# Sums of squares of k and q by products with a block of ones in place of squares with running sums, with a new order of both mixing stages

## The chip, the cores and the metric

One core of a Trainium2 chip. The metric is the device time of one execution in microseconds (us), the median of several runs. The engines are TensorE (PE, products; its loads of weights are PEld), VectorE (DVE), ScalarE (ACT), GpSimd (POOL) and SyncE (SP), which issues the transfers.

## What is computed

Two layers of a decoder trunk over 512 positions of width 1024, in fp32. Each layer first mixes positions by three groups of heads that share one projection in and one out, then runs a gated feed-forward part:

```python
for i in range(DEPTH):
    h = rms_norm(x, attn_pre_norm[i])
    z = h @ w_in[i]
    aq, ak, av, conv_u, gdn_qkv, gdn_gate, gdn_a, gdn_b = jnp.split(z, offsets, axis=-1)
    y_attn = dilated_attention_mixer(aq, ak, av, positions)
    y_conv = conformer_conv_mixer(conv_u, ...)
    y_gdn = gated_deltanet_mixer(gdn_qkv, gdn_gate, gdn_a, gdn_b, ...)
    mix = jnp.concatenate([y_attn, y_conv, y_gdn], axis=-1)
    x = x + rms_norm(mix @ w_out[i], attn_post_norm[i])
    h = rms_norm(x, ffn_pre_norm[i])
    f = (jax.nn.silu(h @ w_gate[i]) * (h @ w_up[i])) @ w_down[i]
    x = x + rms_norm(f, ffn_post_norm[i])
```

The change is in the gated delta rule (4 heads of 128 channels). There k and q pass a short convolution over positions, and each position's vector is scaled to length one:

```python
def l2_normalize(t):
    return t * lax.rsqrt(jnp.sum(t * t, axis=-1, keepdims=True) + L2_EPS)
```

The sums of squares that this needs, one for each position and head, are what the change computes in another way.

## The kernel before, in words

**Layout.** Activations lie channel by channel: a tile has 128 channels as partitions and 512 positions. Dense products take a block of weights of 128x128 against 128x512 of activations; each is done as three products of rounded and remaining parts (h0h with wh, h0h with wl, h0l with wh, for instance). Weights come in units of four blocks, in one fixed order: SP issues the transfer (wr, 256 KB), ACT casts the rounded part (wh), DVE, for some units POOL, subtracts the rest (wl). A unit is twelve products of 128x512.

**The order.** The code does not run as it is written. Every operation is recorded in a plan (`add`, L310) with a cost (`cost`, L267); `forward` (L420) then simulates the engines and writes out one static order for each, always taking the ready operation of highest rank. A rank is the longest path to the end, in which each engine's durations are stretched by the table STRETCH (one for each layer, L143), plus a bonus of the segment (tables BONUS and DENSE, L140 and L141). `issue` (L607) issues that order, so nearly every instruction has line 625. Queues of SP run in the order written. Two things are added by the plan itself: loads of ACT's function tables (L622) where the next function needs another table, and dummies, products `fill` of 128x256 (L1472), where PE has nothing ready and had little work in the time just before.

**A layer's mixing stage.** Its segments are K, Q, V (the delta rule's three inputs), S (its chain over chunks), O (its output), A and B (attention), C (convolution), G (gates) and W (a part of the out-projection, run early). For each head K takes a projection z, `short_conv` (tile kT), four transposes of kT into PSUM (pkt), the sums of squares (`sum_squares`, L1027), and a copy of pkt to SBUF (ktok). From all heads' sums ssk come rk and lrk, from these the rows of decay (prw, pbc, em) and the gram products pkk. The sums acm of their blocks are negated on ACT (acn), go out by two transfers (rows) and come back by 16 transfers as aext, 16 partitions each. DVE then solves a triangular system in 16 steps (sbt, pext), which ends with the last pext. K4 and K5 (tm, pc, c, pd, inner) and the chain S (pvn, pks, pso) follow. In segment Q each head's qT was transposed only for its squares (pqt), then ssq, rq and the rows of q follow. The attention turns its inputs by 4 times 4 transfers between tiles in SBUF (azs) with tables (tab) for the rotation; its last products pao go through DVE (ao) and transposes (paT) into the out-projection.

**The sums before.** For a head, `sum_squares` takes the four 128x128 blocks of the transposes in PSUM, positions as partitions, and ACT squares each and sums it along the row into one column of ssk or ssq (`accum_out`). Each such activation is followed in the records by a read of the accumulator.

Of the kernel before, what the change touches and what calls it, by code (L numbers as in the profile page):

```python
# [11 lines left out]
AF = mybir.ActivationFunctionType  # L12
# [4 lines left out]
S = 512  # L17
# [5 lines left out]
NC = S // 128  # L23
# [3 lines left out]
Q0, K0, V0, U0, G0, GG0, AB0 = 0, 256, 512, 768, 1280, 2816, 3328  # L27
# [109 lines left out]

BONUS = [{'K': 8577.3, 'K1': 1744957.2, 'K2': 999490.1, 'K7': 1081252.3, 'K3': 487102.8, 'K4': -30177.1, 'K5': 114036.9, 'C1': -967277.0, 'Q': 241547.0, 'Q1': 493634.3, 'V': 1059007.4, 'A': 180739.3, 'A1': 662680.2, 'A2': 504358.5, 'S0': 448057.0, 'S1': 509056.5, 'S2': 672779.4, 'S3': 1764589.9, 'O0': 452154.1, 'O1': 482497.0, 'O2': -115387.4, 'O3': 645125.1, 'B3': -55969.7, 'G3': 362503.2, 'C0': -73387.1, 'CN': 684240.7, 'G1': -1321750.9, 'B1': -352050.7, 'B2': -146055.8, 'G2': -444738.8, 'G0': -655720.9, 'B0': -644551.8, 'W': 1406690.3}, {'K': 437659.4, 'K1': 8288.2, 'K2': -21573.9, 'K7': -232713.7, 'K3': 265981.0, 'K4': 64171.9, 'K5': -138460.3, 'Q': -61445.2, 'Q1': -134753.1, 'C1': -196798.2, 'V': 282017.6, 'S0': 956554.0, 'S1': 1194914.1, 'S2': 160050.7, 'S3': 572915.2, 'O0': 624293.1, 'O1': 698094.8, 'O2': -189061.5, 'O3': 501707.8, 'C0': -124334.4, 'CN': 708987.6, 'A': -1560620.8, 'A1': -523695.9, 'A2': -871924.7, 'G0': 1312117.5, 'G3': 241949.4, 'G1': -1313223.2, 'B1': -215325.5, 'G2': -29759.2, 'B2': 632260.6, 'B0': -902903.6, 'B3': -419790.2, 'W': 853551.8}]  # L140
DENSE = [{'K': 1838801.0, 'K1': 1570972.6, 'K2': 1585654.0, 'K7': 1708264.2, 'K3': 1596435.1, 'K4': 2065165.3, 'K5': 1653043.4, 'C1': 2619907.9, 'Q': 639660.4, 'Q1': 623713.0, 'V': -184996.8, 'A': -509056.1, 'A1': -146920.5, 'A2': -488748.4, 'S0': 1317670.9, 'S1': 14477.9, 'S2': 1190644.3, 'S3': 869876.2, 'O0': 602389.2, 'O1': 1207172.3, 'O2': 939331.5, 'O3': 1308009.2, 'B3': -401133.5, 'G3': -21773.3, 'C0': 227567.6, 'CN': -61979.2, 'G1': -372988.3, 'B1': -346176.6, 'B2': -521887.3, 'G2': -365397.0, 'G0': 146413.7, 'B0': 870828.5, 'W': 1037753.1}, {'K': -301790.3, 'K1': -182758.9, 'K2': 1541.0, 'K7': -116696.3, 'K3': 157311.4, 'K4': -227839.6, 'K5': -215982.6, 'Q': -387096.1, 'Q1': 580637.9, 'C1': 26292.9, 'V': 63698.0, 'S0': 100432.3, 'S1': 142318.5, 'S2': 9579.0, 'S3': 420199.1, 'O0': -549345.1, 'O1': -33017.9, 'O2': -638243.5, 'O3': -260264.6, 'C0': 708601.5, 'CN': 579740.9, 'A': -274083.2, 'A1': 249147.9, 'A2': -28643.0, 'G0': -192252.3, 'G3': 500853.9, 'G1': -6303.9, 'B1': 496445.6, 'G2': 490543.7, 'B2': 208435.8, 'B0': -219860.5, 'B3': 165475.0, 'W': 294526.2}]  # L141

STRETCH = [{'PE': 0.1589, 'ACT': 1.5061, 'DVE': 0.9834, 'POOL': 0.0}, {'PE': 0.7128, 'ACT': 2.5956, 'DVE': 2.4432, 'POOL': 0.1292}]  # L143
QUOTA = {'z': 8, 'cm': 2, 'as': 6, 'scm': 2}
TUNE = {'wtop': 1, 'wbonus': 0.0, 'stick': 4000, 'force': 0, 'spread': 2.8, 'low': 2900, 'fill': 5000, 'warm': 12, 'early': 0, 'hib': 2000.0, 'raw': 4, 'half': 12000.0, 'taps': 14, 'plo': 4, 'hold': 1000, 'passes': 0, 'S': 78, 'P': 7, 'Q': 5, 'ahead': 5, 'more': 6, 'n_out': 4, 'n_ffn': 6, 'n_down': 2, 'n_in': 8}

# [111 lines left out]
class Plan:  # L258
# [8 lines left out]
    def cost(self, op, eng, name, outs, ins, kw):  # L267
        if eng == "SP":
            v = (outs + ins)[0]
            op.data = (v.p1 - v.p0) * v.size * 4 / 360  # L270
            if ins and ins[0].tail:
                op.data *= TUNE["spread"]
            return 475
        o = outs[0]
        if eng == "PE":
            if name == "transpose":
                return 62 if ins[0].p1 - ins[0].p0 <= 64 else 112
            w, m = ins[0], ins[1]
            if w.buf.dt == F32R:
                return max(112, 13 + m.size * 0.4167)  # L280
            k, c = w.p1 - w.p0, w.size
            if k == 64 and c == 128:
                return 110 + 0.84 * m.size
            if max(k, c, m.size) <= 64:
                return 62 if max(k, c, m.size) <= 32 else 114
            return max(224, m.size * 1.676)
        n = max([v.size for v in ins] + [o.size])
        psum = any(v.buf.pool.kind == "PSUM" for v in outs + ins)
        if eng == "ACT":
            d = FIXED[eng] + 0.832 * n - 42 * psum  # L290
            d += 93 * sum(isinstance(kw.get(x), View) for x in ("scale", "bias"))
            d += 93 * ("accum_out" in kw)
            return d
        if eng == "DVE":
            per = 1.042
            scalars = op.args[2:4] if name in ("tensor_scalar", "scalar_tensor_tensor") else ()
            if name == "scalar_tensor_tensor":
                scalars = scalars[:1]
            if name in ("tensor_scalar", "tensor_copy", "memset") and not psum:
                per = 0.521  # L300
            if name == "reciprocal":
                per = 8.3
            if name == "tensor_reduce":
                per = 1.8
            ptr = any(isinstance(v, View) for v in scalars)
            return FIXED[eng] + per * n + 9 * ("accum_out" in kw) + 61 * ptr
        per = 3.28 if name == "tensor_copy" else 1.0 if name == "memset" else 4.19 if name == "tensor_scalar" else 2.1
        return FIXED[eng] + per * n
# [319 lines left out]
def trunk(nc, tc, xT, wst, wab, par, con, big, out, depth=DEPTH, dbg=None):  # L628
# [3 lines left out]
    V, A, G, T, SP = (plan.engine(e) for e in ("DVE", "ACT", "POOL", "PE", "SP"))  # L632
    with ExitStack() as ctx:
# [12 lines left out]
        def slot(shape, dt=F32, name="s"):  # L646
            t = slots.tile(shape, dt, name)
            if name in QUOTA:
                t.buf.quota = (name, QUOTA[name])
            return t  # L650
# [4 lines left out]
        def bank(shape=(128, S), name="pb"):  # L655
            t = banks.tile(shape, F32, name)
            if name in QUOTA:
                t.buf.quota = (name, QUOTA[name])
            return t
# [33 lines left out]
        ones = cn[:, C_ONE:C_ONE + 128]  # L693
# [211 lines left out]
        for layer in range(depth):  # L905
# [42 lines left out]
            for seg in SEGMENTS[layer]:  # L948
# [5 lines left out]
                if seg == "K":  # L954
# [66 lines left out]
                    def token_major(src, name):  # L1021
                        ps = bank((128, NC, 128), name=name)
                        for n in range(NC):
                            T.transpose(ps[:, n], src[:, 128 * n:128 * (n + 1)], ident)
                        return ps

                    def sum_squares(ps, dst):  # L1027
                        junk = slot([128, NC, 128], name="junk")
                        for n in range(NC):
                            A.activation(junk[:, n], ps[:, n], AF.Square, accum_out=dst[:, n, :])  # L1030

                    s8r = table(B_S8, "s8", True)

# [2 lines left out]
                    kT, ktok, kkp = [], [], []  # L1036
                    ssk = small([128, NC, 4], "ssk")
                    for hd in range(NH):
                        kT.append(short_conv(project(), 1, hd))
                        ps = token_major(kT[hd], "pkt")  # L1040
                        sum_squares(ps, ssk[:, :, hd:hd + 1])
                        t = slot([128, NC, 128], name="ktok")
                        A.copy(t, ps)
                        ktok.append(t)
# [163 lines left out]
                if seg == "Q":  # L1208

                    qT = []  # L1210
                    ssq = small([128, NC, 4], "ssq")
                    for hd in range(NH):
                        qT.append(short_conv(project(), 0, hd))
                        sum_squares(token_major(qT[hd], "pqt"), ssq[:, :, hd:hd + 1])
                    stage("Q1")
                    rq = small([128, NC, 4], "rq")
                    colq = small([128, NC, 4], "colq")
                    small_rstd(rq, ssq, 1.0, [128, NC, 4], colq)
                    V.scalar_tensor_tensor(colq, colq, -0.5 * math.log(128.0), gcen, op0=OP.add, op1=OP.add)
                    rqe = small([128, NC, 4], "rqe")  # L1220
                    V.scalar_tensor_tensor(rqe, rq, 128.0 ** -0.5, eg, op0=OP.mult, op1=OP.mult)
                    rowq = rows_of(colq, "q")
                    iT = []
                    for hd in range(NH):
                        eq, last = decay(rowq, hd, 1, "eq", inner[:, 1, hd])
                        V.tensor_tensor(eq, gram(kT[hd], qT[hd], "pkq", last), eq, op=OP.mult)
                        iT.append(eq)
                    show("iT0", iT[0])
# [320 lines left out]
```

## Time and profile before

| | |
|---|---|
| median of 3 runs | 1343.43 us (1342.97 to 1344.2) |
| the profiled execution's own time | 1345.2 us |
| its span | 1343.4 us |
| granted clock of TensorE, mean | 0.987 |
| moved by the transfers | 118.50 MB, mean 88 GB/s |
| dense products pmm, share of the chain that ended last | 79% |
| splits wl on DVE | 378, 261.1 us busy |
| casts wh on ACT | 400, 227.6 us busy |

The chain that ended last is followed back from the last instruction, at each step to what released it. In groups of instructions, a row names line, engine, operation, output and inputs, shape and count; then the busy time, the mean of one in ns, and the idle time of the engine just before them with what ended it. In pieces of the timeline, a row holds the start in us from the span's start, the length, the engine and what ran; a bracket holds the idle time before it and what ended that.

Layer 0 runs its mixing stage from some 20 to 255 us and layer 1 from some 690 to 925; between and behind them stand the out-projections and the feed-forward parts.

### The profile page before, as it was taken

What the parts mean: (1) busy time and instruction counts of PE and PEld (TensorE: products, weight loads), DVE (VectorE), ACT (ScalarE), POOL (GpSimd) and SP (SyncE); (2) the same over time, 40 slices, a digit from 0 to 9 for tenths busy, and PEclk for the clock granted to TensorE, in tenths of its full rate; (3) what the DMA queues carried; (4) which work ended last, traced back from release to release, by engine and by line L of the source; (5) the groups of instructions that cost most, each with busy time, mean ns of one, the idle gap of its engine ahead of it and who ended that gap; (6) DMA issues with size and microseconds to landing.
All of it is one profiled execution on the core that took longest, in us unless ns stands there. A gap on an engine that the chain in (4) does not pass through costs nothing.

```text
span 1343.4 us, 20505 instructions
## 1 busy us (share of the span) xinstructions
PE 1314.9 (98%) x7501; PEld 1130.4 (84%) x7501; DVE 824.4 (61%) x1731; ACT 641.5 (48%) x1515; POOL 169.6 (13%) x134
## 2 busy tenths in 40 slices
PE   9999999999999999999999999999999999999996
PEld 8988779789888888878999888878898888888886
DVE  7686989669433444724497999774874334455324
ACT  5785368756222222524358777656642222253321
POOL 1086131100000000000001476310000000000000
PEclk9999989999999999999999979999999999999998
DMA  6064200423323231332301510405133222213311
GB/s 250 9 158 124 89 2 25 141 64 103 94 87 102 89 92 55 109 112 93 116 28 43 155 33 25 141 24 163 43 118 94 98 91 87 88 46 125 108 42 63
DMA packets 64437, 118.50 MB, mean 88 GB/s; under 512 B 8016, under 2 KB 8784, under 8 KB 64336
## 3 DMA queue, kind: packets, MB, share of 16 engines
q1 hardware_dynamic: 64336, 117.19, 28.1%
q8 instruction: 59, 0.97, 0.3%
q14 instruction: 42, 0.34, 0.1%
HBM read 112.70 MB, written 2.36 MB: 86 GB/s over the span
## 4 chain that ended last, share of the span: by engine, by line
PE 89%; DVE 6%; ACT 3%; DMA 1%; issue 1%; POOL 0%; SPq 0%; DVEq 0%; ACTq 0%; POOLq 0%
PE pmm L625 79%; PE pao L625 1%; DVE ca L625 1%; PE pas L625 1%; PE pss L625 1%; PE pso L625 1%; PE pap L625 1%; PE pc L625 1%; PE pkq L625 1%; PE pab L625 1%; PE pd L625 1%; PE pbc L625 1%; DMA x<-in_xT_dram 0%; ACT junk L625 0%; DVE sct L625 0%
## 5 line engine op out<-in xcount | busy, mean ns | idle before, releaser
L625 DVE TENSOR_TENSOR wl<-wr,wh 128x512 fp32r<-128x512 f32 x378 | 261.1, 723 | 77.0 <-ACT wh L625 65.6
L625 ACT CAST wh<-wr 128x512 fp32r<-128x512 f32 x400 | 227.6, 618 | 56.7 <-PE pmm L625 37.6
L625 ACT ACTIVATE g<-g 128x512 f32<-128x512 f32 (+1 forms) x50 | 28.4, 580 | 306.7 <-DVE g L625 306.6
L625 DVE TENSOR_TENSOR g<-pmm,rst 128x512 f32<-128x512 f32 (+1 forms) x50 | 30.8, 625 | 214.0 <-PE pmm L625 213.9
L625 PE MATMUL pmm<-gl,wh 128*128 128x512 f32 (+1 forms) x440 | 124.7, 347 | 0.0
L625 PE MATMUL pmm<-gh,wh 128*128 128x512 f32 (+1 forms) x280 | 92.5, 348 | 1.1 <-ACT gh L625 1.1
L625 PE MATMUL pmm<-gh,wl 128*128 128x512 f32 (+1 forms) x280 | 92.5, 347 | 0.0
L625 PEld LDWEIGHTS pmm<-gl,wh 128*128 128x128 f32 x440 | 71.3, 189 | 10.4 <-DVE gl L625 0.4
L625 POOL TENSOR_TENSOR ca<-ca,cm 128x510 f32<-128x510 f32 (+12 forms) x52 | 72.5, 1395 | 32.2 <-ACT cm L625 29.4
L625 POOL TENSOR_TENSOR abd<-em,cn 128x512 f32<-128x512 f32 x8 | 10.5, 1341 | 516.6 <-PE pbc L625 462.9
L625 DVE TENSOR_TENSOR g<-pmm,g 128x512 f32<-128x512 f32 (+1 forms) x50 | 31.0, 625 | 64.1 <-PE pmm L625 62.7
L625 PE MATMUL pmm<-h0h,wh 128*128 128x512 f32 (+1 forms) x168 | 61.3, 367 | 3.2 <-ACT h0h L625 2.4
L625 PE MATMUL pmm<-h0h,wl 128*128 128x512 f32 (+1 forms) x168 | 60.2, 361 | 3.0 <-DVE wl L625 2.9
L625 PE MATMUL pmm<-h1h,wh 128*128 128x512 f32 (+1 forms) x168 | 60.2, 359 | 0.0
L625 PE MATMUL pmm<-h7h,wl 128*128 128x512 f32 (+1 forms) x168 | 60.0, 358 | 0.0
L625 PE MATMUL pmm<-h2h,wl 128*128 128x512 f32 (+1 forms) x168 | 60.0, 358 | 0.0
L625 PE MATMUL pmm<-h1h,wl 128*128 128x512 f32 (+1 forms) x168 | 60.0, 358 | 0.0
L625 PE MATMUL pmm<-h3h,wh 128*128 128x512 f32 (+1 forms) x168 | 59.9, 358 | 0.0
L625 PE MATMUL pmm<-h7h,wh 128*128 128x512 f32 (+1 forms) x168 | 59.9, 357 | 0.0
L625 PE MATMUL pmm<-h2h,wh 128*128 128x512 f32 (+1 forms) x168 | 59.9, 357 | 0.0
L625 PE MATMUL pmm<-h5h,wh 128*128 128x512 f32 (+1 forms) x168 | 59.8, 358 | 0.0
L625 PEld LDWEIGHTS pmm<-gh,wh 128*128 128x128 f32 x280 | 52.9, 189 | 8.2 <-ACT gh L625 1.7
(420 smaller groups left out, 3620.7 us busy)
## 6 DMA issues: line engine op xcount, KB each, us to landing
wr<-in_wst_dram SPq DMA_DIRECT2D x400, 256.0 KB, 2.7
azs<-z SPq DMA_DIRECT2D x32, 64.0 KB, 2.0
out_dram<-x SPq DMA_DIRECT2D x8, 256.0 KB, 2.1
aext<-rows SPq DMA_DIRECT2D x16, 120.0 KB, 5.0
x<-in_xT_dram SPq DMA_DIRECT2D x3, 512.0 KB, 6.7
tab<-in_big_dram SPq DMA_DIRECT2D x6, 256.0 KB, 4.5
aext<-rows SPq DMA_DIRECT2D x16, 56.0 KB, 2.4
cn<-in_con_dram SPq DMA_DIRECT2D x1, 524.0 KB, 8.3
```

Source lines behind the costliest of these rows:

```text
L625: getattr(engines[op.eng], op.name)(*[real(v) for v in op.args], **{k: real(v) for k, v in op.kw.items()})
```

## The change

`sum_squares` now takes the tile kT or qT itself, channels as partitions. ACT squares it in one instruction of 128x512; four products then sum over the channels: each block of 128 positions of the squares against eight columns of a block of ones, into a tile psq of PSUM with eight equal columns; DVE copies the first column to ssk or ssq. The transposes of q (pqt) are dropped, since only the squares read them; those of k stay, since ktok is copied from them. In the plan, the issue of a transfer between two tiles in SBUF costs 620 in place of 475. The tables BONUS, DENSE and STRETCH have other numbers in all places, of which the third is shown.

```diff
-STRETCH = [{'PE': 0.1589, 'ACT': 1.5061, 'DVE': 0.9834, 'POOL': 0.0}, {'PE': 0.7128, 'ACT': 2.5956, 'DVE': 2.4432, 'POOL': 0.1292}]
+STRETCH = [{'PE': 0.1138, 'ACT': 0.723, 'DVE': 1.8624, 'POOL': 0.0}, {'PE': 0.7301, 'ACT': 0.8941, 'DVE': 1.9472, 'POOL': 0.709}]
...
-            return 475
+            return 620 if all(v.buf.pool.kind == "SBUF" for v in outs + ins) else 475
...
-                    def sum_squares(ps, dst):
-                        junk = slot([128, NC, 128], name="junk")
+                    def sum_squares(src, dst):
+
+                        sq = slot([128, S], name="junk")
+                        A.activation(sq, src, AF.Square)
+                        ps = bank((128, NC, 8), name="psq")
                         for n in range(NC):
-                            A.activation(junk[:, n], ps[:, n], AF.Square, accum_out=dst[:, n, :])
+                            T.matmul(ps[:, n], sq[:, 128 * n:128 * (n + 1)], ones[:, 0:8], start=True, stop=True)
+                        V.tensor_copy(dst, ps[:, :, 0:1])
...
                         ps = token_major(kT[hd], "pkt")
-                        sum_squares(ps, ssk[:, :, hd:hd + 1])
+                        sum_squares(kT[hd], ssk[:, :, hd:hd + 1])
...
-                        sum_squares(token_major(qT[hd], "pqt"), ssq[:, :, hd:hd + 1])
+                        sum_squares(qT[hd], ssq[:, :, hd:hd + 1])
```

The order of both mixing stages is planned anew by this. Three places of it follow; a row is an instruction of an engine in its order, with output, inputs, shape, and how many stand in a row.

On PE, in segment K of layer 0, where the transposes pkt and gram products pkk of the first head stand (a piece of the difference, - before, + now; a product of fp32 counts once here and shows as two records in a trace):

```order
 L625 MATMUL pkt<-cn,kT_636 128x128 x4
-L625 MATMUL pkk<-kT_636 128x128 x4
+L625 MATMUL pkk<-kT_636 128x128
+L625 MATMUL psq<-cn,junk 128x8 x8
+L625 MATMUL pkk<-kT_636 128x128 x3
 L625 MATMUL pmm<-h7h,wh 128x256
 L625 MATMUL pmm<-h7h,wl 128x256
```

Two heads' sums, eight products psq, now stand between the gram products of the first head.

On SP, in layer 0, from the last of the first units of weights (wr) to the first rotary transfers (azs); rows and aext are the two stages of the solve's input. Before:

```order
L625 DMA s_832<-in_big_dram 128x512
L625 DMA wr<-in_wst_dram 128x512
L625 DMA rows_1034<-acn 128x128
L625 DMA rows_1039<-acn 128x128
L625 DMA wr<-in_wst_dram 128x512 x3
L625 DMA aext<-rows_1034 16x896 x8
L625 DMA aext<-rows_1039 16x1920 x8
L625 DMA wr<-in_wst_dram 128x512 x12
L625 DMA azs<-z 32x512 x4
L625 DMA wr<-in_wst_dram 128x512 x3
L625 DMA azs<-z 32x512 x3
L625 DMA tab<-in_big_dram 128x512
```

And now:

```order
L625 DMA s_813<-in_big_dram 128x512
L625 DMA wr<-in_wst_dram 128x512 x2
L625 DMA rows_1037<-acn 128x128
L625 DMA rows_1043<-acn 128x128
L625 DMA aext<-rows_1037 16x896 x8
L625 DMA aext<-rows_1043 16x1920 x8
L625 DMA wr<-in_wst_dram 128x512 x17
L625 DMA azs<-z 32x512 x4
L625 DMA wr<-in_wst_dram 128x512
L625 DMA tab<-in_big_dram 128x512
L625 DMA azs<-z 32x512 x3
L625 DMA tab<-in_big_dram 128x512
```

No unit stands between rows and aext any more and one more ahead of rows: 22 units in all are ahead of aext for 24. The first four azs have 39 units ahead of them for 36, and the first table comes ahead of the second group of azs.

On PE, at the end of layer 0's attention, the last transposes paT into the out-projection (pap and pao are the attention's own products, pot a transpose of the delta rule's output, mah an attention output as an input of the out-projection). Before:

```order
L625 MATMUL pao<-av_1972,asp 128x64
L625 MATMUL pot<-cn,ot 128x128
L625 MATMUL pmm<-h0h,wh 128x512
L625 MATMUL pmm<-h0h,wl 128x512
L625 MATMUL pmm<-h0l,wh 128x512
L625 MATMUL pmm<-h1h,wh 128x512
L625 MATMUL pmm<-h1h,wl 128x512
L625 MATMUL pmm<-h1l,wh 128x512
L625 MATMUL pmm<-h2h,wh 128x512
L625 MATMUL paT<-cn,ao 128x128 x2
L625 MATMUL pmm<-h2h,wl 128x512
```

And now:

```order
L1476 MATMUL fill<-mkr,idr 128x256 x5
L625 MATMUL paT<-cn,ao 128x128 x2
L625 MATMUL pap<-cn,as 128x128
L1476 MATMUL fill<-mkr,idr 128x256 x6
L625 MATMUL pap<-cn,as 128x128
L625 MATMUL pao<-av_2476,asp 128x64 x2
L625 MATMUL pap<-cn,as 128x128
L625 MATMUL pao<-av_2476,asp 128x64 x2
L1476 MATMUL fill<-mkr,idr 128x256 x7
L625 MATMUL paT<-cn,ao 128x128 x2
L1476 MATMUL fill<-mkr,idr 128x256 x5
L625 MATMUL pmm<-mah_2853,wh 128x512
```

Dense products stood beside the last steps of the attention; now the attention stands alone there with dummies, and the dense products have moved ahead of it.

In the whole program PE has 64 products psq more, 32 transposes pqt less and 97 dummies for 61, of these 60 for 14 in layer 0's mixing stage and 6 for 12 in layer 1's; ACT has 16 squares of 128x512 for 64 of 128x128 and 33 table loads for 27; DVE has 16 copies more; POOL and SP have the same instructions in another order.

More of the change, by code (lines that the diff above doesn't have):

```diff
@@ L131, in constants @@
     return con, big
-BONUS = [{'K': 8577.3, 'K1': 1744957.2, 'K2': 999490.1, 'K7': 1081252.3, 'K3': 487102.8, 'K4': -30177.1, 'K5': 114036.9, 'C1': -967277.0, 'Q': 241547.0, 'Q1': 493634.3, 'V': 1059007.4, 'A': 180739.3, 'A1': 662680.2, 'A2': 504358.5, 'S0': 448057.0, 'S1': 509056.5, 'S2': 672779.4, 'S3': 1764589.9, 'O0': 452154.1, 'O1': 482497.0, 'O2': -115387.4, 'O3': 645125.1, 'B3': -55969.7, 'G3': 362503.2, 'C0': -73387.1, 'CN': 684240.7, 'G1': -1321750.9, 'B1': -352050.7, 'B2': -146055.8, 'G2': -444738.8, 'G0': -655720.9, 'B0': -644551.8, 'W': 1406690.3}, {'K': 437659.4, 'K1': 8288.2, 'K2': -21573.9, 'K7': -232713.7, 'K3': 265981.0, 'K4': 64171.9, 'K5': -138460.3, 'Q': -61445.2, 'Q1': -134753.1, 'C1': -196798.2, 'V': 282017.6, 'S0': 956554.0, 'S1': 1194914.1, 'S2': 160050.7, 'S3': 572915.2, 'O0': 624293.1, 'O1': 698094.8, 'O2': -189061.5, 'O3': 501707.8, 'C0': -124334.4, 'CN': 708987.6, 'A': -1560620.8, 'A1': -523695.9, 'A2': -871924.7, 'G0': 1312117.5, 'G3': 241949.4, 'G1': -1313223.2, 'B1': -215325.5, 'G2': -29759.2, 'B2': 632260.6, 'B0': -902903.6, 'B3': -419790.2, 'W': 853551.8}]
@@ L141 @@
-DENSE = [{'K': 1838801.0, 'K1': 1570972.6, 'K2': 1585654.0, 'K7': 1708264.2, 'K3': 1596435.1, 'K4': 2065165.3, 'K5': 1653043.4, 'C1': 2619907.9, 'Q': 639660.4, 'Q1': 623713.0, 'V': -184996.8, 'A': -509056.1, 'A1': -146920.5, 'A2': -488748.4, 'S0': 1317670.9, 'S1': 14477.9, 'S2': 1190644.3, 'S3': 869876.2, 'O0': 602389.2, 'O1': 1207172.3, 'O2': 939331.5, 'O3': 1308009.2, 'B3': -401133.5, 'G3': -21773.3, 'C0': 227567.6, 'CN': -61979.2, 'G1': -372988.3, 'B1': -346176.6, 'B2': -521887.3, 'G2': -365397.0, 'G0': 146413.7, 'B0': 870828.5, 'W': 1037753.1}, {'K': -301790.3, 'K1': -182758.9, 'K2': 1541.0, 'K7': -116696.3, 'K3': 157311.4, 'K4': -227839.6, 'K5': -215982.6, 'Q': -387096.1, 'Q1': 580637.9, 'C1': 26292.9, 'V': 63698.0, 'S0': 100432.3, 'S1': 142318.5, 'S2': 9579.0, 'S3': 420199.1, 'O0': -549345.1, 'O1': -33017.9, 'O2': -638243.5, 'O3': -260264.6, 'C0': 708601.5, 'CN': 579740.9, 'A': -274083.2, 'A1': 249147.9, 'A2': -28643.0, 'G0': -192252.3, 'G3': 500853.9, 'G1': -6303.9, 'B1': 496445.6, 'G2': 490543.7, 'B2': 208435.8, 'B0': -219860.5, 'B3': 165475.0, 'W': 294526.2}]
@@ L143 @@
-STRETCH = [{'PE': 0.1589, 'ACT': 1.5061, 'DVE': 0.9834, 'POOL': 0.0}, {'PE': 0.7128, 'ACT': 2.5956, 'DVE': 2.4432, 'POOL': 0.1292}]
+BONUS = [{'K': 13715.4, 'K1': 1555096.9, 'K2': 1258241.8, 'K7': 568984.7, 'K3': 425985.3, 'K4': 248721.4, 'K5': 266769.2, 'C1': -1469054.9, 'Q': 372947.3, 'Q1': 543037.0, 'V': 1139191.0, 'A': 188546.2, 'A1': 804174.4, 'A2': 480453.1, 'S0': 204919.0, 'S1': 1278306.7, 'S2': 527140.7, 'S3': 1453468.7, 'O0': 37638.8, 'O1': 413103.5, 'O2': -521366.8, 'O3': 325599.8, 'B3': -199767.8, 'G3': 464845.7, 'C0': -34775.2, 'CN': 794680.9, 'G1': -1003853.4, 'B1': -606436.9, 'B2': -404190.5, 'G2': -641825.2, 'G0': -567806.8, 'B0': -867416.3, 'W': 1755851.3}, {'K': 955837.8, 'K1': 31898.0, 'K2': 9926.6, 'K7': -1072882.9, 'K3': 576461.1, 'K4': 157402.6, 'K5': -125594.9, 'Q': -76543.8, 'Q1': -137170.3, 'C1': -444782.0, 'V': 343676.9, 'S0': 1495245.4, 'S1': 1241595.5, 'S2': 78199.1, 'S3': 1095137.7, 'O0': 383570.6, 'O1': 592491.3, 'O2': 49270.8, 'O3': -40989.5, 'C0': 45798.8, 'CN': 349595.8, 'A': 278092.3, 'A1': -669299.0, 'A2': -831949.7, 'G0': 1446308.1, 'G3': -105376.0, 'G1': -961004.4, 'B1': 69296.1, 'G2': 319506.7, 'B2': 453001.5, 'B0': -803156.3, 'B3': -503667.7, 'W': 690004.0}]
@@ new lines @@
+DENSE = [{'K': 1760413.4, 'K1': 1672962.2, 'K2': 1559163.1, 'K7': 1511974.3, 'K3': 1707988.9, 'K4': 2108395.9, 'K5': 1762296.3, 'C1': 2540967.5, 'Q': 663324.5, 'Q1': 565533.8, 'V': -105317.3, 'A': -432444.2, 'A1': 17485.7, 'A2': -334487.2, 'S0': 1256396.8, 'S1': 180726.2, 'S2': 1165799.8, 'S3': 860526.0, 'O0': 583223.2, 'O1': 1213326.1, 'O2': 902416.2, 'O3': 1321850.5, 'B3': -398636.8, 'G3': -18686.4, 'C0': 280057.4, 'CN': 94842.4, 'G1': -387953.0, 'B1': -424956.3, 'B2': -532451.5, 'G2': -436648.5, 'G0': 74198.8, 'B0': 977566.1, 'W': 951545.8}, {'K': -168737.9, 'K1': -173108.1, 'K2': 86688.4, 'K7': -62615.8, 'K3': 14931.7, 'K4': -354881.0, 'K5': -226195.9, 'Q': -301289.7, 'Q1': 607413.5, 'C1': -266139.0, 'V': 28744.5, 'S0': 319985.3, 'S1': 264409.1, 'S2': 42135.7, 'S3': 263711.4, 'O0': -555102.9, 'O1': -40798.9, 'O2': -665643.9, 'O3': -281270.5, 'C0': 510222.6, 'CN': 523240.5, 'A': -447493.8, 'A1': 351211.8, 'A2': -105162.7, 'G0': -69718.6, 'G3': 355495.9, 'G1': -51646.9, 'B1': 554237.7, 'G2': 416511.4, 'B2': 281959.9, 'B0': -180792.1, 'B3': 172346.1, 'W': 518253.4}]
```

## The prediction

> **What bounds the kernel now.** I read the page's first part (busy time of each engine), then the chain that ended last, then the busy time by stretch of the span.
>
> ```profile
> PE 1314.9 (98%) x7501; PEld 1130.4 (84%) x7501; DVE 824.4 (61%) x1731; ACT 641.5 (48%) x1515; POOL 169.6 (13%) x134
> PE 89%; DVE 6%; ACT 3%; DMA 1%; issue 1%; POOL 0%; SPq 0%; DVEq 0%; ACTq 0%; POOLq 0%
> 20.00:130.00 110.00, 110.00 (x672) 97.04 (x671) 84.56 (x186) 72.99 (x183) 47.49 (x37) 1.00 0.34 96
> 130.00:160.00 30.00, 27.11 (x118) 22.07 (x117) 26.29 (x49) 8.84 (x15) 9.49 (x7) 0.94 0.44 129
> 160.00:220.00 60.00, 57.87 (x564) 50.70 (x563) 53.44 (x138) 43.96 (x154) 18.01 (x15) 0.94 0.02 5
> 220.00:255.00 35.00, 33.97 (x199) 28.10 (x198) 29.90 (x91) 30.29 (x89) 3.85 (x3) 1.00 0.34 108
> 255.00:690.00 435.00, 431.55 (x2280) 373.08 (x2280) 221.23 (x424) 163.69 (x326) 1.34 (x1) 1.00 0.30 92
> 690.00:780.00 90.00, 89.58 (x559) 79.03 (x558) 78.11 (x195) 66.80 (x184) 25.18 (x19) 1.00 0.28 77
> 780.00:840.00 60.00, 57.57 (x516) 51.34 (x515) 58.56 (x101) 45.26 (x126) 42.41 (x31) 0.86 0.09 28
> 870.00:925.00 55.00, 53.91 (x296) 42.06 (x295) 35.52 (x94) 31.05 (x76) 7.51 (x6) 1.00 0.26 84
> ```
>
> The rows by stretch hold: the stretch and its length, the busy time of PE, PEld, DVE, ACT and POOL (each with its count), the granted clock, the DMA share and GB/s. Two things are to be seen. PE is busy nearly always, so whatever the change gives to PE costs its length unless it lands where PE has no work. And there are only three places where PE loses time: 130 to 255 and 780 to 840, where the delta-rule chain and the attention run and DVE is fuller than elsewhere, and a little at 870 to 925. How much is lost there: in 130 to 160 idle 2.9 and throttled 0.06 x 30 = 1.8; in 160 to 220 idle 2.1 and throttled 0.06 x 60 = 3.6; in 220 to 255 idle 1.0; so 11.4 us in layer 0. In 780 to 840 idle 2.4 and throttled 0.14 x 60 = 8.4; so 10.8 in layer 1. These **22 us are the pool** from which a better order can win; the rest of the span, 435 us from 255 to 690 among it, holds hardly any loss.
>
> **Products.** 64 products with the block of ones come (16 calls, 4 each), and 32 transposes of q go. A product of fp32 shows as two records. No product with 128 rows of moving data and 8 columns is in the trace, so I bound it by the nearest.
>
> ```profile
> 46.84 0.89 PE pkk L625 x8
> 38.28 0.98 PE pabt L625 x8
> 56.50 0.80 PE pg L625 x6
> 744.75 0.88 PE pqt L625 x8
> 326.80 268.33 PE pmm L625 x1238
> ```
>
> These are pieces of the chain: start, length, what, and how many records. pkk, the gram product, loads a 128x128 block of fp32 as the new product does: 0.111 us a record. pabt (8 columns) takes 0.122 and pg (16 columns, 128 rows) 0.133. A transpose of q takes 0.11. Upper end: 128 records x 0.133 = 17.1. For the lower end, a dense product of 512 columns takes 268.33 / 1238 = 0.217; so from 128 to 512 columns a record grows by 0.106, 0.00028 a column; 120 columns fewer than pkk would give 0.078, or 10.0 for all. I take pkk's 0.111, since the two rows with few columns lie above it and not below: 14.2. Less the transposes, 32 x 0.11 = 3.5, that is **+10.7** (6.5 to 13.5), half in each layer. All of it is on the engine that is 98% busy, and in layer 1 all of it is ahead of the chain.
>
> Against this stands a rule of the Trainium skill, "TensorE: Matmul & The Clock Gate", section "Wait — 56ns, not 53.3ns?": from start to start a product takes at least about 25 ns, however few columns it has. By that alone 128 records would cost 3.2 us, as an estimate, and the term would be 0 in place of 10.7; but it counts columns, and the records of pg and pabt above, at 0.13 and 0.12 with 16 and 8 columns, do not follow it where each product brings a block of its own to load.
>
> **ACT.** 64 squares of 128x128 with their sums go, 16 squares of 128x512 come, and the table loads go from 27 to 33.
>
> ```profile
> 711.78 2.58 ACT junk L625 x20
> L625 ACT ACTIVATE osq<-o 128x512 f32<-128x512 f32 x6 | 3.8, 630 | 2.5 <-DVE o L625 2.5
> L622 ACT ACT_TABLE_LOAD x26 | 33.4, 1283 | 0.5
> 52.38 0.68 ACT L625 COPY ktok<-pkt 128x512 f32<-128x512 f32 x1
> 53.08 1.28 ACT L622 ACT_TABLE_LOAD   x1
> 54.37 0.22 ACT L625 ACTIVATE rk<-ms__734 128x16 f32<-128x16 f32 x1
> ```
>
> The chain's piece is ten squares with their ten reads: 0.26 each, so 64 x 0.26 = 16.5 go. A square of 128x512 between SBUF tiles is in the trace under another name, 0.63: 16 x 0.63 = 10.1. Six loads x 1.283 = 7.7. Sum +1.3: ACT is not relieved. With ACT busy for 48% this lies beside PE's work; only where acn waits for ACT does it count, below. Uncovered, it would cost its 1.3.
>
> The Trainium skill, "ScalarE: Activation LUTs", section "What ACT_TABLE_LOAD costs", gives a switch about 1.28 us for the load and about 1.38 for a drain ahead of it. The last three rows above show no drain: the copy ends at 53.06, the load starts at 53.08 and the next activation at 54.37. By the page, as an estimate, six switches would take 16.0 and not 7.7, and acn would come some 2.8 us later than I reckon below; I go by the rows.
>
> **DVE.** 16 copies of psq to ssk or ssq come.
>
> ```profile
> L625 DVE COPY xab<-pabt 128x16 f32<-128x16 f32 x2 | 0.3, 164 | 0.0
> ```
>
> 16 x 0.16 = 2.6 us, taken as hidden: the 4 of k in layer 0 and all 8 of layer 1 lie in 20 to 130 and 690 to 780, where PE has dense work and waits for none of them. Uncovered it is 2.6.
>
> **The wait for the first weights behind aext, layer 0.** Before, 24 units of weights are issued ahead of the 16 transfers of aext; after, 22. PE thus has two units less in hand while SP issues aext.
>
> ```profile
> 71.79 0.67 ACT L625 ACTIVATE acn<-acm 128x128 f32<-128x128 f32 x2 [0.39 <-DVE acm L625]
> 74.64 7.32 SPq L625 DMA_DIRECT2D aext<-rows  x16
> wr<-in_wst_dram SPq DMA_DIRECT2D x13, 256.0 KB, 5.2
> 86.31 0.39 PE L625 MATMUL pmm<-h0h,wh 128*128 128x512 f32 x1
> ```
>
> PE first uses the 23rd unit at 86.31. In the new order 5.2 us more of PE work (products of k, pieces moved forward) lie ahead of that use, with the durations of this trace: 91.5. When does the unit come? Along ACT's new order acn stands 3.6 us later (two more table loads ahead of it, 2.6, and moved pieces). The three units that were issued between rows and aext fitted into the wait for rows, so aext's issue ends at 81.96 + 3.6 = 85.6; the unit behind it lands in 5.2 (the DMA view of 70 to 95, median), is cast in 0.6 and split in 0.7: 92.1. So PE is short by 0.6 for the first unit, and the later ones follow as fast as aext's transfers leave room. I take **+2** (0 if acn isn't later, 4 if the second unit is late as well). 16 dummies stand in the order just there, 16 x 0.19 = 3.0 at most by the group's row below.
>
> ```profile
> L1472 PE MATMUL fill<-mkr,idr 128*128 128x256 f32 x61 | 11.6, 317 | 0.0
> ```
>
> **The rotary transfers, layer 0.** Before, they hold up three units, and then the tables:
>
> ```profile
> 128.39 2.42 SPq L625 DMA_DIRECT2D azs<-z  x4
> 132.66 1.03 DVE L625 TENSOR_TENSOR azs<-azs,tab 128x512 f32<-128x512 f32 x1 [3.97 <-DMA tab<-in_big_dram]
> 135.32 1.75 DVE L625 TENSOR_TENSOR azs<-azs,tab 128x512 f32<-128x512 f32 x1
> 137.73 0.79 PE L625 MATMUL pmm<-h0h,wl 128*128 128x512 f32 x1 [2.89 <-DVE wl L625]
> 130.00:140.00 10.00, 7.11 (x27) 5.50 (x26) 7.33 (x8) 1.86 (x3) 6.45 (x5) 0.86 0.61 170
> ```
>
> DVE stands 3.97 us at a table, the split wl waits behind it, and PE idles 2.89 at a clock of 0.86: 2.9 + 1.4 = 4.3. In the plan an issue of azs now counts 620 for 475 (the trace: 2.42 / 4 = 0.6 us), the first group stands behind 39 units for 36, and a table ahead of the second group. I take **-3.5** (-4.3 to 0).
>
> **The delta-rule chain and the attention, layer 0.** The new order runs the attention behind the chain, with dense work of the partial out-projection ahead of it; 47 dense products fewer are left behind the last transposes paT (257 before, 210 after), and dummies stand there now.
>
> ```profile
> 151.74:248.77 97.03, 94.88 (x777) 81.54 (x776) 85.44 (x231) 73.78 (x239) 23.22 (x18) 0.96 0.11 34
> 249.12 0.38 PE L625 MATMUL paT<-cn,ao 128*128 128x128 f32 x2
> ```
>
> The row is the stretch from the end of the solve on DVE to the last ao, which paT waits for: DVE is busy for 85.44 of 97.03, 88%. Along the new order DVE has 94.2 us of work between the same two points. At 88% that is 107, from a start some 3 us earlier (the wait of 3.97 above): the last ao comes at 255.7, 7 later, while 47 x 0.227 = 10.7 less is to be done behind it, so -3.8 for layer 0 as a whole. By PE's own work it is +5.3 for products, +2 and -3.5: +3.8. The two accounts lie on both sides; neither is better borne out, and I take their middle, **0** for layer 0 (-8 to +7), which is to say that some 4 us more of the loss after 160 are won back.
>
> **Layer 1.** +5.3 for products. Along the new order DVE has 4.2 us less of work between the first product of the chain and its last scratch tile, in 780 to 840, where DVE is 98% busy (58.56 of 60) and PE loses 10.8; but then the second half of the attention needs about as much DVE work as before. I take **-2** (0 to -5): +3.3.
>
> **Dummies.** They go from 61 to 97; 46 more in layer 0's mixing. Each stands where the plan has no product ready, so I cost them at nothing; if real work is ready there, the 36 cost 36 x 0.19 = 6.8.
>
> **Sum.** 10.7 + 2 - 3.5 - 4 - 2 = +3.2: about 0 in layer 0 and 3.3 in layer 1. The profiled execution took 1345.2 us (span 1343.4), 1.8 above the median of the runs shown, 1343.43; the difference is put on the median: 1343.4 + 3.3 = **1347**. A difference under 0.2%, 2.7 us, can't be told from none here.
>
> **Rivals.**
> A, faster: the new order wins back most of the pool. The place is the chain in both layers, 150 to 255 and 780 to 840; the price of the products and of aext's wait is 10.7 + 2 = 12.7; from 15.4 of the 22 us on, the kernel is faster by more than 2.7. With 18 to 20 won, -5 to -7: about 1338. For it: DVE's 4.2 us less in layer 1, at a place where DVE sets the time and the clock is 0.86; the account by DVE in layer 0. Against it: 46 more dummies in layer 0 say that PE has less ready there, not more. The page's 25 ns would give the same 10.7 by another way, about 1337.
> B, no change: 10 to 15 are won back, or the product costs its lower end: 1341 to 1346. That the change doesn't do what it says belongs here: ACT isn't relieved by it at all.
> C, slower by much: the dummies stand where work is ready (6.8), the units behind aext come late twice (4), and the gain stays at 9.5: 10.7 + 4 + 6.8 - 9.5 = +12, about 1355.
> F, the forecast: products paid in full, half of them won back: 1346.2 to 1352.
>
> **Chances.** F 0.36, A 0.30 (0.03 of it by the page's rule), B 0.22, C 0.12. For the signs: faster 0.30, same 0.22, slower 0.48. The likeliest case gives 1347, alone 1346 to 1352. The range reaches from A's far end, 1335, with some 0.08 below it, to C's middle, 1356, with some 0.06 above.
>
> **What would show it.** psq records at 0.11 each (right), at 0.08 or 0.03 (the sum falls by 4 to 10). PE idle of 1 to 4 us at about 92, waiting for wh or wl. No wait of DVE for tab near 130 and the clock at 1.00 there. The last paT of layer 0 at 253 to 258, and the following stretch of dense products 10 us shorter. In layer 1 the clock of 60 us from the chain's start above 0.86. The prediction is wrong if the clock in both chain stretches rises to 0.95 or more (A), or if dummies run while a unit already lies ready (C).

## The result and the profile after

The changed kernel takes 1367.95 us (median of 4 runs, 1366.47 to 1369.46) against 1343.53 before: a ratio of 1.0179, 95% interval 1.0166 to 1.0192. It is 24.4 us slower; 1347 was forecast, 1356 the upper end of the range. Its profiled execution has a span of 1365.7, so 22.3 more than the one before; the sums below are made against these 22.3.

The first part of the page of the changed kernel, and its busy time by stretch, in the stretches of before (columns as there):

```profile
PE 1335.5 (98%) x7633; PEld 1147.7 (84%) x7633; DVE 828.8 (61%) x1747; ACT 642.6 (47%) x1409; POOL 167.5 (12%) x134
20.00:130.00 110.00, 109.31 (x688) 97.29 (x687) 87.74 (x195) 75.28 (x157) 46.47 (x36) 0.98 0.30 87
130.00:160.00 30.00, 29.17 (x128) 23.35 (x127) 28.34 (x47) 9.60 (x16) 9.74 (x6) 0.94 0.43 138
160.00:220.00 60.00, 58.86 (x539) 50.99 (x538) 55.98 (x129) 36.34 (x108) 17.87 (x15) 0.94 0.06 17
220.00:255.00 35.00, 33.41 (x203) 27.70 (x202) 24.81 (x83) 30.14 (x85) 3.85 (x3) 1.00 0.16 46
255.00:280.00 25.00, 23.64 (x134) 19.52 (x133) 9.84 (x24) 14.77 (x33) 1.29 (x1) 1.00 0.40 127
780.00:840.00 60.00, 58.53 (x455) 49.99 (x453) 44.82 (x76) 48.20 (x97) 38.47 (x31) 0.83 0.13 36
```

PE is as full as before, and there is nothing here that looks like 22 us of waiting. That is what makes this page hard to read: PE is also busy with products that were not there before, and with dummies. Two things are new. In 255 to 280 DVE has as little to do as before (9.84 of 25 us, 9.88 before), but the attention still runs there, whose last transposes started at 249.2 before, and ACT is busy for 14.77 (11.70 before). And the clock is 0.98 in 20 to 130, where it was 1.00.

Where the time went is told by marks in the program: the last transposes paT (end of layer 0's mixing stage) and the first gate product's g on DVE (start of layer 0's feed-forward part). The rows are those of the two tiles in layer 0: count, shortest, median and longest duration in ns, first and last start in us. First before, then the changed kernel:

```profile
L625 PE MATMUL paT<-cn,ao x8: 270/272/279, 219.9 to 249.2; 128*128 128x128 f32 x8
L625 DVE TENSOR_TENSOR g<-pmm,rst x25: 406/691/692, 315.5 to 534.4; 128x512 f32<-128x512 f32 x19, 128x256 f32<-128x256 f32 x6
```

```profile
L625 PE MATMUL paT<-cn,ao x8: 270/272/300, 229.7 to 276.5; 128*128 128x128 f32 x8
L625 DVE TENSOR_TENSOR g<-pmm,rst x25: 414/691/692, 329.3 to 548.8; 128x512 f32<-128x512 f32 x19, 128x256 f32<-128x256 f32 x6
```

The last paT comes 27.3 later, and the feed-forward part 13.8 later, since less dense work is left behind paT. The first products pab of the changed kernel come 0.2 later already. So **layer 0 costs some 13.6 us and layer 1 the other 8.6**; 0 and 3.3 were forecast.

A sum over stretches of 5 us, over both mixing stages to the start of what follows, divides this up. Idle is the stretch less PE's busy time; clock is the busy time by what the granted clock lacks of 1; dummies is the time from the start of a row of dummies to the start of the next product; psq and pqt likewise.

| us, layer 0 / layer 1 | idle | clock | dummies | psq | pqt |
|---|---|---|---|---|---|
| before | 7.8 / 4.7 | 4.2 / 8.3 | 9.2 / 5.3 | - | 1.6 / 1.5 |
| changed | 6.5 / 6.8 | 6.8 / 9.5 | 13.2 / 4.0 | 6.7 / 6.6 | - |

Products: +13.3 - 3.1 = 10.2. Idle, clock and dummies together: 39.5 before, 46.8 now, +7.3. That makes 17.5 of 22.3; the other 4.8 is time in which PE is busy with work that both kernels have, and this account doesn't divide it further.

### The profile page after: what moved, and what is told of

It reads as the page before. It is cut to its first block, busy times and chain, and to the rows that moved or that the text cites. A ratio compares the mean times of both kernels' runs of the same rounds, so it can differ in the third digit from the quotient of the medians.

```text
span 1365.7 us, 20690 instructions
## 1 busy us (share of the span) xinstructions
PE 1335.5 (98%) x7633; PEld 1147.7 (84%) x7633; DVE 828.8 (61%) x1747; ACT 642.6 (47%) x1409; POOL 167.5 (12%) x134
## 5 line engine op out<-in xcount | busy, mean ns | idle before, releaser
L625 ACT ACTIVATE g<-g 128x512 f32<-128x512 f32 (+1 forms) x50 | 28.4, 580 | 307.8 <-DVE g L625 307.6
L625 POOL TENSOR_TENSOR abd<-em,cn 128x512 f32<-128x512 f32 x8 | 10.2, 1301 | 515.2 <-PE pbc L625 511.3
L625 DVE TENSOR_TENSOR g<-pmm,g 128x512 f32<-128x512 f32 (+1 forms) x50 | 31.0, 625 | 62.2 <-PE pmm L625 60.6
L625 PE MATMUL pmm<-h3l,wh 128*128 128x512 f32 (+1 forms) x168 | 60.3, 359 | 0.0
L625 PE MATMUL pmm<-h2l,wh 128*128 128x512 f32 (+1 forms) x168 | 60.2, 359 | 0.0
L625 PE MATMUL pmm<-h0l,wh 128*128 128x512 f32 (+1 forms) x168 | 60.1, 359 | 0.0
L625 PE MATMUL pmm<-h1l,wh 128*128 128x512 f32 (+1 forms) x168 | 59.9, 358 | 0.0
```

The source lines that it names most:

```text
L625: getattr(engines[op.eng], op.name)(*[real(v) for v in op.args], **{k: real(v) for k, v in op.kw.items()})
```

## Experiments

Each run had the kernel before timed beside it on the same chip (1344.9 to 1345.3; beside the changed kernel it took 1343.5). A difference of some 2 us between the median of a run here and that of the changed kernel therefore says little by itself. Sums over stretches come from one profiled execution of each kernel.

**1. The sums alone.** The kernel before with the new `sum_squares`, the old tables and the issue cost 475:

```diff
-            return 620 if all(v.buf.pool.kind == "SBUF" for v in outs + ins) else 475
+            return 475
...
-STRETCH = [{'PE': 0.1138, 'ACT': 0.723, ...
+STRETCH = [{'PE': 0.1589, 'ACT': 1.5061, ...
```

(The diff is against the changed kernel; BONUS and DENSE go back as well.)

> The kernel before with the new sum_squares alone (old tables, issue cost 475); the plan is made anew. P (products are the main cost, 0.22 us each on PE, transposes saved): 10.7 us slower than before, about 1354. O (the order made by the new tables is the main cost): 4 us or less, 1343 to 1348, since the products then cost only what the plan can't hide. If it comes out above 1360, the old tables don't suit the new sums and neither theory is told apart by it.

Measured: 1358.41, ratio 1.0110 (1.0086 to 1.0134), 13.1 slower. That is more than the 10.7 of theory P and far from theory O, and 9.5 less than the changed kernel. Its layer 0 is 4.8 later at the first g (320.3 for 315.5), where the changed kernel's is 13.8 later. So the products are there in both, and what the changed kernel has on top lies in layer 0's new order; layer 1 costs about as much in both (7.9 and 8.6 by the spans).

**2. The new tables alone**, with the squares on ACT and 475.

> The kernel before with the new tables alone (old squares on ACT, issue cost 475). P: within 5 us of before, 1339 to 1349, since the order neither wins nor loses much. O: the order's loss stays without the products, +8 to +15, 1351 to 1358.

Measured: 1416.99, ratio 1.0536 (1.0518 to 1.0554). Neither theory had this. Layer 1 has 355 dummies here, 26 before: these tables make a bad order for the squares. That doesn't say what the tables cost with the new sums, and I draw nothing else from it.

**3. The issue cost 620 alone.**

> The kernel before with the issue cost 620 alone. Both theories: the wait of DVE for a table near 130 us (3.97 us, PE idle 2.89) goes or shrinks; if this is all, -2 to -4, 1339 to 1341. If the plan moves more than the transfers of layer 0, anything from -5 to +10 is possible, and the place of the gain or loss tells which.

Measured: 1343.92, ratio 0.9989 (0.9980 to 0.9999). DVE's wait for a table, 3.97 us before, is gone from the waits of 120 to 160, but a wait of 3.0 for the projection's product has come (z for pmm), and the first g comes at 317.6, 2.1 later than before. The wait went as forecast, but the layer didn't become shorter by it.

**4. Each product twice**, in the changed kernel's own order:

```diff
             op = self.ops[i]
+            if op.eng == "PE" and op.name == "matmul" and op.args[0].buf.name == "psq":
+                getattr(engines[op.eng], op.name)(*[real(v) for v in op.args], **{k: real(v) for k, v in op.kw.items()})
```

> The changed kernel in its own order, each of the 64 products with ones issued twice (the second overwrites the first with the same values). P: the 64 more cost 64 x 0.22 = 14.2 us, 1382. O with products hidden behind other waits: under 7, 1368 to 1375. If a product costs only its columns (0.03 a record): 3 to 4, about 1371.

Measured: 1392.08, ratio 1.0342 (1.0319 to 1.0366): 24 more than the changed kernel, where 14.2 was expected. The profiled execution was the fastest of the four, and its span is 20.2 longer. In it the time in psq grows by 16.3 (13.3 to 29.6), about what their length gives; but the clock's loss in the mixing stages grows too, from 16.3 to 25.1. Together that is 25.1, so a part of it was hidden. A stretch behind the second doubled row of psq (it starts at 55.9 and lasts 3.5):

```profile
62.00:66.00 4.00, 4.00 (x20) 3.68 (x20) 2.50 (x16) 2.91 (x12) 0.00 (x0) 0.50 0.00 0
```

PE runs at half its clock with 4.00 of 4.00 us busy. Here a row of such products costs its length and then a slower clock for what stands behind it.

**5. No dummies**, the order otherwise the same:

```diff
             if i == "fill":
-                self.fill(engines["PE"])
                 continue
```

> The changed kernel in its own order without the 97 dummies. If they run where real work is ready (they cost their 0.12 to 0.19 us each), 36 more than before's cost 4 to 7 and all 97 cost 12 to 18: 1350 to 1356. If they only fill waits, as the prediction took it, the time stays within 3 of the changed kernel's 1368, the idle time of PE grows by what they took, and a lower granted clock behind them would show as a loss.

Measured: 1373.80, ratio 1.0215 (1.0200 to 1.0230): 5.9 above the changed kernel's median, more than the 3 allowed for, and not below it. Idle time in layer 0 grows from 6.5 to 14.4 and the clock's loss from 6.8 to 11.3; the clock is at 0.50 from 274.4 to 281.3 and from 318.8 to 325.6, in and behind the places where dummies stood. The dummies cover waits, and keep the clock up there. So the 29 of them at the end of layer 0's attention are in sum not a cost, they mark one: PE waits there.

**6. The products with 128 columns of ones** in place of 8, in the same order (a product's `work` in the plan is set to the old 28, so that nothing moves):

```diff
-                        ps = bank((128, NC, 8), name="psq")
+                        ps = bank((128, NC, 128), name="psq")
...
-                            T.matmul(ps[:, n], sq[:, 128 * n:128 * (n + 1)], ones[:, 0:8], start=True, stop=True)
+                            T.matmul(ps[:, n], sq[:, 128 * n:128 * (n + 1)], ones[:, 0:128], start=True, stop=True)
```

> The changed kernel in the same order, each product with ones given 128 columns of ones in place of 8 (same loads of weights, the first column is still the one copied). Theory C (rows of short products let the granted clock fall behind them: 0.65 at 56 to 60 in the changed kernel): the record stays at 0.11 to 0.12, the clock at 56 to 64 stays at 1.00, and the time falls by 1.5 to 3, to about 1365. Theory P (only the length of the products counts): the same time or up to 128 x 0.01 longer, 1368 to 1370, and the clock is as before.

Measured: 1365.65, ratio 1.0152 (1.0135 to 1.0169). The same stretch behind the k products, first the changed kernel, then this one:

```profile
56.00:60.00 4.00, 4.00 (x27) 3.69 (x26) 2.69 (x21) 2.48 (x12) 0.00 (x0) 0.65 0.00 0
```

```profile
56.00:60.00 4.00, 3.66 (x33) 3.41 (x33) 3.16 (x23) 2.44 (x11) 0.00 (x0) 1.00 0.00 0
```

With 16 times the columns the clock stays at 1.00, behind the q products at 154 to 162 too (0.77 and 0.80 in the changed kernel); 33 records run in place of 27. A mean over 4 us hides how the clock falls: to 0.50, for a whole stretch of 3.41 us (in run 4 for twice that, 59.6 to 66.4). The changed kernel around that stretch, then run 5, where PE's order is the same up to 94 us:

```profile
53.78:57.19 3.41, 3.41 (x33) 3.41 (x32) 1.50 (x11) 2.30 (x7) 0.00 (x0) 1.00 0.00 0
57.19:60.60 3.41, 3.41 (x17) 3.10 (x17) 2.14 (x16) 2.42 (x10) 0.00 (x0) 0.50 0.00 0
60.60:64.01 3.41, 3.41 (x28) 3.32 (x28) 1.16 (x3) 3.41 (x13) 0.00 (x0) 1.00 0.00 0
```

```profile
52.58:55.99 3.41, 3.41 (x33) 3.41 (x31) 0.83 (x7) 2.83 (x6) 0.00 (x0) 1.00 0.02 5
55.99:59.40 3.41, 3.07 (x28) 2.82 (x27) 2.62 (x20) 1.93 (x10) 0.00 (x0) 1.00 0.00 0
```

Run 5 has the same row of 8 columns at 53.9, and the clock stays at 1.00 behind it. It does so behind the rows of k in runs 1 and 8, and behind the changed kernel's own rows at 47.1 and 721.6. With 128 columns, here and in run 10, no row of these products has a fall behind it. So by these executions few columns are needed for the fall, but they are not enough. What else decides, perhaps where a row falls against the stretches of 3.41 us, was not tried. And the cost is small: of the 3.5 us of clock that layer 0 wins, 1.2 come back as idle time, the first g comes 1.4 earlier (327.9), and the medians of the two kernels lie 2.3 apart, with intervals that just overlap. That is a cost of 2 us or so, and not the bulk.

**7. A late order.** The changed kernel with some numbers of the tables altered (among them BONUS of layer 0's K5 from 266769 to -7095 and O3 from 325600 to -23789; they were drawn at random, and those kept that the plan itself took to be shorter). PE's order in layer 0 stays the same up to segment K4.

> The changed kernel with a few numbers of its tables altered, so that layer 0 keeps its order up to segment K4 (the sums, the aext transfers, the table loads ahead of them are the same) and has another one from there; layer 1 gets another order too. Theory T (the extra of layer 0 is the attention's end, where exp and silu alternate on ACT, six table loads stand from 241 to 267, and PE runs 29 dummies): the last paT of layer 0 comes at 262 to 270 in place of 277, the feed-forward part of layer 0 starts at 319 to 323 in place of 329, and the kernel takes 1355 to 1360. Theory E (the extra of layer 0 comes before K4: products, clock, aext, ACT): layer 0 stays at 327 or more, and the kernel at 1364 or more.

Measured: 1361.36, ratio 1.0117 (1.0100 to 1.0133). Its rows of paT and g in layer 0:

```profile
L625 PE MATMUL paT<-cn,ao x8: 270/272/329, 229.6 to 270.3; 128*128 128x128 f32 x8
L625 DVE TENSOR_TENSOR g<-pmm,rst x25: 408/691/692, 323.4 to 541.9; 128x512 f32<-128x512 f32 x19, 128x256 f32<-128x256 f32 x6
```

This execution began 1.1 later (segment K's first products, pab, end at 38.0 for 36.9), so layer 0 is 7.0 us shorter than the changed kernel's, 322.3 to 329.3, with all of the products, the table loads and the aext transfers ahead of it unchanged. 329 became 323.4, at the edge of what theory T gave; the last paT, at 270.3, and the time lie just beyond it, 0.3 and 1.4 us. The chain (its last pvn) ends at nearly the same place in both, at 216.8 and 217.3 (218.4 less the 1.1), so the gain lies behind it. What differs is the attention's end. The rows hold the busy time of the dense products pmm and of what reads them (PE, PEld, DVE and ACT, then clock, DMA share and GB/s) in the last 12 us ahead of the end of the last paT: before, in the changed kernel, and in the late order.

```profile
237.50:249.50 12.00, 8.56 (x32) 5.99 (x33) 0.84 (x2) 0.00 (x0) 1.00 0.35 101
264.80:276.80 12.00, 3.25 (x12) 2.10 (x12) 0.10 (x1) 0.00 (x0) 1.00 0.50 164
258.55:270.55 12.00, 8.95 (x34) 5.60 (x32) 0.69 (x1) 0.00 (x0) 1.00 0.68 206
```

The changed kernel has 12 dense products there for 32 and 34; 22 fewer than the late order, at 0.227 each, are 5.0 of the 7.0 us. In the changed kernel, ACT and DVE there (start, length; a bracket holds the idle time ahead of a row and what ended it):

```profile
254.07 1.28 ACT L622 ACT_TABLE_LOAD   x1
256.52 1.28 ACT L622 ACT_TABLE_LOAD   x1
260.41 1.28 ACT L622 ACT_TABLE_LOAD   x1
264.93 0.63 ACT L625 ACTIVATE gs<-z 128x512 f32<-128x512 f32 x1 [3.24 <-DVE z L625]
265.84 1.28 ACT L622 ACT_TABLE_LOAD   x1
267.14 0.40 ACT L625 ACTIVATE as<-as,amm 128x128 f32<-128x128 f32 x1
264.21 0.69 DVE L625 SCALAR_TENSOR_TENSOR z<-pmm,rst 128x512 f32<-128x512 f32 x1 [3.46 <-PE pmm L625]
```

Read it from ACT: the table for the gate's silu is loaded at 260.41, then ACT stands 3.24 us for the last gate's z, which DVE can only make when PE has done its dense products at 264; then the table for exp is loaded again, and only at 267.14 come exps of the attention's last blocks. DVE too stands 3.46 for that z; their scores, whose products pas had started at 246.2 at the latest, are queued behind it until 265.4. The attention's end waits in two in-order queues behind one gate. This is read from the trace: the late order moves many operations from K4 on, and no run moved that gate alone. In the late order ACT's last exp starts at 255.8 and the gates come behind it:

```profile
251.75 1.28 ACT L622 ACT_TABLE_LOAD   x1
255.75 0.39 ACT L625 ACTIVATE as<-as,amm 128x128 f32<-128x128 f32 x1
256.76 1.28 ACT L622 ACT_TABLE_LOAD   x1
258.06 0.63 ACT L625 ACTIVATE gs<-z 128x512 f32<-128x512 f32 x1
```

Layer 1, ordered anew as well, gives some 3 us back in this execution.

**8 and 9. Other tables, with and without the new sums.** Both start from the kernel before with 475; numbers of the tables are altered as in the run above, 17 and 18 of them, first with the new `sum_squares`, then with the squares on ACT.

> The kernel before with the new sum_squares alone (issue cost 475) and the old tables with some numbers altered, in both layers. P (the products cost their 10.2 us whatever the order): not below 1352, 8 to 13 over before. If an order hides them: below 1350.

> The kernel before, squares on ACT as they were, with some numbers of its tables altered in the same way as in the run with the new sums: the counterpart of that run. P: 8 to 13 us faster than that run, 1338 to 1345. If orders chosen in this way bring nothing on the chip: 1345 or more.

Measured: 1348.78 with the new sums, ratio 1.0034 (1.0021 to 1.0048), and 1342.30 with the squares, ratio 0.9979 (0.9965 to 0.9992). So the same sums, with 13.8 us of psq, can stand in an order that is only 3.9 us slower than before: idle, clock and dummies are 28.4 us there, 39.5 before and 46.8 in the changed kernel. The counterpart is 6.5 faster, less than the 8 to 13 that theory P gave; each is one order of many, so 6.5 is no exact price of the sums. The run with the squares is the fastest of all here, and faster than before by a little more than can be told from nothing.

**10. The late order with 128 columns.**

> The run with the late order, each product with ones given 128 columns, in the same order. Theory C (rows of short products lower the clock behind them): clock loss in layer 0 falls by 3, the time by 1 to 3 against that run. P: no change.

Measured: 1361.63, ratio 1.0118 (1.0103 to 1.0134), as without them. Theory C fails here: behind the products the clock stays at 1.00, but it is at 0.50 from 184.1 to 190.9, in the chain, where the run with 8 columns has 1.00, and the clock's loss in layer 0 is 3.4 in both.

## Why the prediction was wrong

**The bound and the products: right.** PE was and is the bound. 128 records of psq at 0.111 less 32 transposes were to give +10.7; measured +10.2 (the table above). One reading on the way was wrong: 0.133 for pg and 0.122 for pabt are lengths of pieces that hold the whole last record, of some 0.26; from start to start they are 0.11 each (six pg from 56.49 to 57.04), as pkk's are. So the upper end of 17.1 had no ground, and the value taken, 0.111, had more for it than was said. The row of the tile in the changed kernel, and the stretch in which the second row of products ends (54.0 to 55.8):

```profile
L625 PE MATMUL psq<-cn,junk x128: 170/256/277, 47.1 to 760.9; 128*128 128x8 f32 x128
```

```profile
54.00:58.00 4.00, 4.00 (x35) 4.00 (x34) 2.19 (x17) 2.40 (x8) 0.00 (x0) 0.90 0.00 0
```

The durations of overlapping records (256 ns) are not their spacing; by starts, 13.3 us / 128 = 0.104 each. The Trainium skill's page "TensorE: Matmul & The Clock Gate" (section "Wait — 56ns, not 53.3ns?") gives about 25 ns as the least from start to start; these products stay at four times that, as the rows of pg and pabt had said.

**The clock behind the products: missed.** The stretch above already holds the start of the fall, at 0.90 in the mean. The prediction priced psq by its length alone; run 4 shows a price beyond it, and run 6 that it goes away with more columns. In the changed kernel it was small: the clock's loss is 3.8 more in all, 3.5 of it undone in layer 0 by more columns.

**aext: right in its size.** +2 was forecast, with PE there at 91.5 and the unit at about 92. PE was there at 94.8 and got it 2.2 us late, its two parts at 95.8 and 97.3; the dummies of that place run in between (PE in the changed kernel's timeline):

```profile
94.80 0.88 PE L1476 MATMUL fill<-mkr,idr 128*128 128x256 f32 x6
95.80 0.50 PE L625 MATMUL pmm<-h0h,wh 128*128 128x512 f32 x1
96.14 1.35 PE L1476 MATMUL fill<-mkr,idr 128*128 128x256 f32 x10
97.33 0.40 PE L625 MATMUL pmm<-h0h,wl 128*128 128x512 f32 x1
```

**The rotary transfers: right where they are, not kept.** -3.5 was forecast; idle and clock in 120 to 150 fall from 3.8 to 0.1, and the wait for a table from 3.97 to 1.08 (DVE in the timeline, then the stretch):

```profile
135.36 0.69 DVE L625 TENSOR_TENSOR azs<-azs,tab 128x512 f32<-128x512 f32 x1 [1.08 <-DMA tab<-in_big_dram]
```

```profile
130.00:140.00 10.00, 9.91 (x44) 7.90 (x43) 8.82 (x15) 2.44 (x4) 6.37 (x4) 1.00 0.63 196
```

Then, in 150 to 200, they rise from 5.4 to 6.2 (150 to 199 before), and the solve ends at 151.7, as before (152.1), not 3 us earlier: its first step (sbt) started 10.7 later, at 84.5 for 73.8, which the prediction didn't follow up to here.

**The chain and the attention of layer 0: here the prediction fell.** Two accounts, +3.8 by PE and -3.8 by DVE, were averaged to 0 for layer 0, which put a win of 4 us behind 160 into the sum. Measured are 13.6. In the sum's own terms, products 5.1, aext 2.2 and the rotary transfers -3.7 make 3.6 of it; where the win of 4 stood, 10.0 were lost. Run 7 wins 7.0 of layer 0 by its order from K4 on, and run 6 some 1.4 of the clock; the rest is open. The account by DVE put the last ao at 255.7, as if DVE's share of 88% went on. The last ao ended at 276.1; from the end of the chain (216.8) to the last paT (276.8) DVE is busy for 37.4 of 60.0 us, where before it was busy for 31.6 of 36.0 (214.5 to 250.5). DVE's work doesn't limit this end: by the trace it waits, as ACT does, for one gate's product behind which both queues stand. The account knew how much work each engine has and not who stands behind whom. That the 46 more dummies in layer 0 were named as evidence against a win, and then priced at nothing, is the same fault: run 5 shows that the dummies cost nothing in sum, run 7 that a wait that they mark does. The PE account, +3.8, was nearer, and lacked just those waits.

**Layer 1: -2 was forecast for its order**; measured 8.6 in all, 5.1 of it products, so its order lost some 3.5 and won nothing; with the old tables (run 1) layer 1 costs 7.9, so most of that isn't special to the new ones. The chain itself did get shorter: from the first to the last pvn it takes 26.6 us for 29.6, and DVE is busy for 23.9 of them, 28.7 before. But the chain starts later, and more is lost ahead of it, in K4 and K5: idle time and clock come to 10.2 from 775.6 to 830.5, and to 7.3 from 770.2 to 806.7 before. The sign that the prediction named, a clock above 0.86 in the 60 us from the first of these products on, came out the other way (0.83 from 776.5 to 836.5). The forecast looked at the chain alone. Which wait ahead of it does this was not tried apart.

**The pool.** The 22 us of idle time and clock left out the dummies, 14.5 us in the mixing stages; with them, and with 25.0 of idle time and clock over the whole of both stages, it was 39.5, and the orders of runs 8 and 9 win 7 to 11 of it. Room for a win was there, and this order didn't take it. ACT's term (+1.3, hidden) plays no part in the sum above except that acn came 5.1 later (3.6 forecast), which aext's term holds.

## What to carry to other kernels

Moving a sum from an engine at 48% to one at 98% costs about its length there unless an order is found that takes it into its waits (3.9 us in run 8, 13.1 in run 1); it is the reverse of what relieves a kernel. When a plan is made anew, count its dummies: here they cost nothing in sum, and each place where they stand is a wait that the plan itself saw. A share of busy time doesn't forecast an attention's end; look in each in-order queue for a late input (here one gate) ahead of work that is ready, above all where ACT must load a table between the two.

## What the runs showed of the hardware

A product of fp32 with 128x128 weights of its own takes 0.104 us a record from start to start with 8 columns and 0.107 with 128 (13.3 and 13.7 us for 128 records, changed kernel and run 6). Rows of such products with 8 columns can lower the granted clock for what follows although PE is 100% busy: to 0.50 for 3.41 us behind 16 records (57.2 to 60.6 in the changed kernel) and for 6.83 us behind 32 (59.6 to 66.4 in run 4). Other rows of 16 have no fall behind them (47.1 in the changed kernel, 53.9 in run 5), and with 128 columns none has (runs 6 and 10). Without the dummies the clock falls in and behind the places where they stood (0.50 from 274.4 to 281.3 and from 318.8 to 325.6, run 5).
